# An encoder layer on one core: attention traced with priority, the input fetched a second time, gate sums and the last weight halves put into other tiles

## The chip, the cores and the metric

The kernel runs on one core of one Trainium2 chip. The metric is the device time of one execution in microseconds. TensorE (PE in the profile) multiplies matrices into PSUM, VectorE (DVE) and ScalarE (ACT) work on tiles element by element, GpSimd (POOL) and SyncE (SP) issue most of the transfers. Each engine has its own queue of instructions and works through it in order; engines wait for one another through semaphores.

## The reference

One layer of an encoder on 256 positions of width 2048, all in float32. A vector `c` sets scales, shifts and gates through one large matrix (`mod`). The layer is a windowed attention (32 query heads, 8 key and value heads of 64, rotary positions, one extra logit per head, the "sink") and an MLP with squared ReLU and 8192 hidden units; each of them is followed by a layer norm over a weighted sum with its input.

```python
c_act = jax.nn.silu(c)
mod = c_act @ mod_w[i] + mod_b[i]
sh_m, sc_m, g_m, sh_f, sc_f, g_f = jnp.split(mod, 6, axis=-1)
hmix = x * (1.0 + sc_m[:, None, :]) + sh_m[:, None, :]
y = windowed_gqa_sink(hmix, positions, attn_w_qkv[j], attn_b_qkv[j], attn_sink[j], attn_w_o[j], attn_b_o[j])
x = layer_norm(DEEPNORM_ALPHA * x + (1.0 + g_m[:, None, :]) * y, ln_mix_g[i], ln_mix_b[i])
hff = x * (1.0 + sc_f[:, None, :]) + sh_f[:, None, :]
y = sq_relu_mlp(hff, mlp_w1[i], mlp_b1[i], mlp_w2[i], mlp_b2[i])
x = layer_norm(DEEPNORM_ALPHA * x + (1.0 + g_f[:, None, :]) * y, ln_mlp_g[i], ln_mlp_b[i])
...
# inside the attention
s = jnp.where(valid[None, :, None, None], s, -jnp.inf)
m = jnp.maximum(jnp.max(s, axis=-1, keepdims=True), sk)
p = jnp.exp(s - m)
p = p / (jnp.sum(p, axis=-1, keepdims=True) + jnp.exp(sk - m))
```

With 256 positions there are two query blocks of 128, and both see all keys inside the window of 128.

## The kernel before

**Precision.** Every large product is split: a weight tile `raw` (128x2048, 1 MB) is rounded to a high part `wh` by ScalarE (L254, two halves of 128x1024 each), and VectorE takes the rest, `wl` = `raw` - `wh` (L225). Activations are split in the same way. A product is then three matmuls (`mm3`, L498 to L500: high x high, high x low, low x high), each with 512 columns. `ff_hidden` does the same with two matmuls (L1042, L1043), as its activations hold both parts side by side.

**The stream of weights.** `class Stream` holds one list of all weight tiles in order of use (`S.plan`). Its entries are either weights of a product, or tiles of the `mod` matrix, which carry a function `use` (`Mod.step`). SP loads them in this order into five buffers (`raws`; at first three more, `raws2`). `S.main()` returns the halves of the next weight tile and `pump` casts ahead of it, by up to five high halves (`NHIGH`); `S.stop` is a place in the list that `pump` does not pass. A `mod` tile is worked off either by TensorE (`quad`, L314) or by VectorE (L352, multiply and add into the tiles `part`).

**Who sets the order.** The functions are traced in a fixed order, and a planner then puts the instructions of each engine in order: among those that are ready at the time that it assumes, the one traced first goes first. A tile of a pool takes a buffer when its first writer is placed, and waits if all are taken; a buffer is free when the last reader of its tile is done.

**Pools.** `gen` has 20 buffers of 128x1024 floats (`g4()`); it holds the input `xs` (4), the projections `acc`, keys, queries, probabilities `P` and their transposes `pT`, attention outputs, hidden activations and more. `gen2` has 6 buffers of the same size (`g4b()`), opened when `raws2` is closed. PSUM has five banks `psa` (products, scores, values), two `pst` (transposes) and one `psm` (sums of `mod`).

**Stages.** First q, k, v are projected, while the input arrives, is transposed (`turn_x`) and modulated. Then come 21 steps, `n` = 0 to 20. In step `n` < 16 a block of four heads and 128 queries has its `scores` (L735, L736 on TensorE; mask and maximum L738, L740, L743, L745 on VectorE; four exponentials L749 and a small one L751 on ScalarE) and is normalised (`normalise`, L757, L758 and four L764); the block before it is transposed (`probs_T`, L774, with two copies L776), and every second step a pair of blocks is multiplied with the values (`values`, L789, cast L791). Four blocks make a group, whose queries are turned by `q_heads` (L703, L705). Beside this each step has one weight tile: the last projections in steps 0 to 3, and from step 5 on the output projection (`project`), which adds into `ys` (L849, L852) and, in its third row, adds the input `xs` (L855, L856). Step 12 makes the gate (`gate`, L391 to L398).

**The MLP** has four blocks of 2048 hidden units. For each, `ff_hidden` makes the hidden activations (in block 0 another loop, L1002 to L1029), and `ff_out` makes four columns of 512 outputs, which are added into the four tiles `ys`: in block 0 with the bias `bf` (L1081), later without (L1083). During block 1 the gate of the MLP is summed by VectorE alone (`m_gf`, L352), into two tiles `part` that are first cleared by POOL and given the bias by a DMA (L334, L335); in block 2 `gate(m_gf)` turns these sums into the gate `g2`. Block 3 ends with the fourth column: its four weight tiles are kept whole (`ws`), so that the first 128 positions can be finished, and normalised (L797 to L813, L1122 to L1129), while the second 128 are multiplied. The halves of its last two weight tiles are `kept`, in g4 tiles.

Of the kernel before, what the change touches and what calls it, by code (L numbers as in the profile page):

```python
# [12 lines left out]
F32R = mybir.dt.float32r  # L13
# [7 lines left out]
S = 256  # L21
NT = S // 128
# [8 lines left out]
BLK = 4  # L31
# [9 lines left out]
NHIGH = 5  # L41
NLOW = 5
VECS = 2
ORDER_ONLY = mybir.DependencyInfo(mybir.DependencyClass.NoSync, mybir.DependencyReason.DATA)


@with_exitstack
def hybrid_kernel(ctx: ExitStack, tc: tile.TileContext, a, out: bass.AP):
    nc = tc.nc
# [22 lines left out]
    def g4(dt=F32):  # L72
        return gen.tile([128, 1024], dt, tag="g4", name="g4")
# [96 lines left out]

        return add

    def bias_all(src, g4=g4):

        b = [g4(), g4()]
        for h in range(2):
            nc.gpsimd.dma_start(b[h], src[:, h * 1024:h * 1024 + 1024].partition_broadcast(128))
        return lambda c: b[c // 2][:, (c % 2) * 512:(c % 2) * 512 + 512]


    class Stream:
# [15 lines left out]
            self.prev = None  # L197
            self.side = {}

        def plan(self, src, use=None, kept=False):  # L200
            self.q.append((src, use, kept))

        def loads(self):
# [17 lines left out]
        def low(self):  # L221
            n = len(self.ls)
            r, kept = self.src[n]
            l = g4(F32R) if kept else wlp.tile([128, 1024], F32R, name="wl")
            self.pinned(nc.vector.tensor_sub(l, r, f32(self.hs[n])))  # L225
            self.ls.append(l)
            if n % 2:
                self.freed(self.of[n])

        def pump(self, vecs, must=0):  # L230

            while len(self.ls) < must or self.at < len(self.q):
                self.loads()
                n = len(self.hs)
                if len(self.ls) < n - 1 and len(self.ls) - self.used < self.nl or len(self.ls) < min(must, n):
                    self.low()
                    continue
                if self.at >= len(self.q) or self.at == self.stop:
                    return
                assert self.at < len(self.raw)  # L240
                src, use, kept = self.q[self.at]
                if use is not None:
                    if not vecs and n >= must:
                        return
                    vecs = max(vecs - 1, 0)
                    use(self.raw[self.at])
                    self.at += 1
                    self.freed(self.at - 1)
                    continue
                if n >= must and (n - self.used >= self.nh or kept):  # L250
                    return
                h = g4(F32R) if kept else whp.tile([128, 1024], F32R, name="wh")
                s = self.raw[self.at][:, n % 2 * 1024:n % 2 * 1024 + 1024]
                self.pinned(nc.scalar.copy(h, s))  # L254
                self.hs.append(h)
                self.src.append((s, kept))
                self.of.append(self.at)
                self.at += n % 2
# [33 lines left out]
    class Mod:  # L292
# [29 lines left out]
        def step(self, raw):  # L322
            w, kc, i = self.w, self.kc, self.i
            if i == 0:
                self.ps = psm.tile([128, 512], F32, name="pm")
            r = raw.rearrange("p (k j n) -> p k j n", k=kc // 2 if self.pairs else kc, j=4)
            self.i += 1
            last = self.i == self.n
            per = 1024 // w
            if i == self.start:  # L330

                self.part = [(g4b if self.whole else g4)() for _ in range(2)]
                for n, p in enumerate(self.part):
                    nc.gpsimd.memset(p, 0.0)  # L334
                    nc.scalar.dma_start(p[0:1], self.bias[:, n * 1024:n * 1024 + 1024])  # L335
            for k in range(kc):
                kt = i * kc + k
                if self.pairs:
                    if k % 2 == 0:
                        cols = [cact[:, kt + j // 2:kt + j // 2 + 1].to_broadcast([128, 32]) for j in range(4)]  # L340
                        self.quad(cols, [r[:, k // 2, j] for j in range(4)], last and k == kc - 2)
                elif i in self.dve:
                    e = min(4 * w, 1024)
                    new = self.part is None
                    if new:
                        self.part = [g4() for _ in range(4 * w // e)]
                    for n, p in enumerate(self.part):
                        s = raw[:, k * 4 * w + n * e:k * 4 * w + n * e + e]
                        if new:
                            nc.vector.tensor_scalar(p[:, :e], s, cact[:, kt:kt + 1], None, op0=OP.mult)  # L350
                        else:
                            nc.vector.scalar_tensor_tensor(p[:, :e], s, cact[:, kt:kt + 1], p[:, :e],  # L352
                                                           op0=OP.mult, op1=OP.add)
                else:
                    stop = last and k == kc - 1 and not self.dve
                    self.quad(cact[:, kt:kt + 1].to_broadcast([128, 32]), [r[:, k, j] for j in range(4)], stop)
            if last and not self.whole:
                if self.dve:
                    self.quad(onesf[:, :32], [self.part[j // per][:, (j % per) * w:(j % per) * w + w]
                                              for j in range(4)], True)  # L360
                self.r = sml.tile([128, 512], F32, name="mrow", bufs=2)
                nc.scalar.copy(self.r[:, :w], self.ps[:, :w])
# [116 lines left out]
    for blk in range(BLK):  # L479
        for f in range(NF):  # L480
            if blk:
                if blk == 1 and f % 2:
                    m_gf.plan()
                S.plan(a["w1b"][(blk - 1) * NF + f])
        for c in range(4):
            for kg in range(4):
                if blk == 1 and kg % 2:
                    m_gf.plan()
                S.plan(a["w2"][blk, c, kg], None, blk == BLK - 1 and c == 3 and kg > 1)


    acc, xts, held, xs = {}, {}, {}, []
# [377 lines left out]
    for h in range(2):  # L870
        qT[0, h] = q_heads(qhl[0], h)

    def mids(n):
        out = []
        if 0 < n <= 16:
            out.append(lambda: probs_T(n - 1))
        if n < 16:
            out.append(lambda: normalise(n))
        return out

    todo = []
# [1 line left out]
    for n in range(21):  # L883
        j, i = n // 4, n % 4
        if n < 16:
            scores(n)
        for f in todo:
            f()
        todo = []
        if n == 1:  # L890
            S.deep = False
        if n == 5:
            assert all(h is raws for h in S.home[S.at:]), "an early buffer is still in use"
        if n + 2 < len(LATE):
            w = qkv(*LATE[n + 2])
        elif n < 5:
            w = iter((0, 1))
        else:
            if n == 5:
                ys, bo = [g4b() for _ in range(4)], bias_all(a["bo"], g4b)  # L900
            w = project((n - 5) // 4, (n - 5) % 4)
        S.vecs(SLOT_FILL.get(n, 0) if len(LATE) - 2 <= n < 5 else 0)
        mid = mids(n)
        if j < 3:
            if i == 0:
                turn = rope(j + 1, 1)
            if i < 3:
                mid.append(lambda: qA.__setitem__(j + 1, next(turn)))
            if i == 2:
                mid.append(lambda: qhl.__setitem__(j + 1, split_q(qA[j + 1])))  # L910
            if i == 3:
                for h in range(2):
                    mid.append(lambda h=h: qT.__setitem__((j + 1, h), q_heads(qhl[j + 1], h)))
        run(w, mid)
        if 0 < n <= 16 and n % 2 == 0:
            todo.append(values(n - 1))
        if n == 12:
            g1 = gate(m_gm)
# [148 lines left out]
        return pss  # L1067

    ys = [g4b() for _ in range(4)]
    bf = bias_all(a["b2"], g4b)  # L1070
    for blk in range(BLK - 1):
        if blk:
            us = ff_hidden(blk)
        for c in range(4):
# [9 lines left out]
            if blk == 1:  # L1084
                for t in range(NT):
                    z = part(xs, t, c)
                    nc.vector.scalar_tensor_tensor(z, z, ALPHA, gb[0], op0=OP.mult, op1=OP.mult)
                    nc.vector.scalar_tensor_tensor(z, gb[1], ALPHA, z, op0=OP.mult, op1=OP.add)

    blk = BLK - 1  # L1090
    us = ff_hidden(blk)
# [120 lines left out]
```

## Time and profile before

| | us |
|---|---|
| runs of the kernel | 1139.51, 1139.80, 1135.54 (median 1139.51) |
| the profiled execution, its own time | 1136.72 |
| its span, first to last instruction | 1135.0 |
| TensorE busy in that span | 1088.9 |
| VectorE, ScalarE, GpSimd busy | 811.0, 546.7, 21.7 |

The profiled execution is one more run with the recorder on; the difference between its time and its span lies around the program. Busy time of TensorE counts pipelined matmuls, so a busy TensorE is not necessarily at its peak. A row of the profile names the line of the kernel, the engine, the operation and output<-inputs; an arrow at the end of a row gives the idle time of that engine just before it and what ended it. "Granted clock" (PEclk) is the share of the full TensorE clock that the chip allowed in that stretch.

### The profile page before, as it was taken

Reading aid. Unit: us, or ns where it says so; the run is one execution under the profiler, and the core shown is the slowest. Engines: PE = TensorE matmul, PEld = TensorE weight load, DVE = VectorE, ACT = ScalarE, POOL = GpSimd, SP = SyncE. Lnnn points to the kernel's source line nnn. Section 1 sums busy time; section 2 is a strip of 40 time slices with the busy share of each in tenths; the row PEclk is TensorE's granted clock in tenths of the full one; section 3 lists DMA queues with packets and bytes.
Section 4 is the critical chain, followed back from the end, with each engine's and each line's share of the span. In section 5 each row is a group of like instructions: output and inputs, shape, how many; then the busy total and the mean of one; then the engine's idle time right before and its main releaser. Section 6 shows DMA issues by size and latency. Waiting matters only on the chain.

```text
span 1135.0 us, 15765 instructions
## 1 busy us (share of the span) xinstructions
PE 1088.9 (96%) x6250; PEld 880.2 (78%) x6250; DVE 811.0 (71%) x1121; ACT 546.7 (48%) x852; POOL 21.7 (2%) x40
## 2 busy tenths in 40 slices
PE   8889999799999999999999999999999999999994
PEld 6657667466677699988888887878888888888883
DVE  5587896778899878765577888746666556665656
ACT  5333445676775455553444543335444344444431
POOL 2000000000000000000000010000000000000001
PEclk9999999999999999999999999999999999999997
DMA  9999995656886798655578788854555555557512
GB/s 374 419 420 418 421 392 196 253 186 255 322 305 258 276 366 313 207 187 186 196 290 296 263 303 319 303 206 155 187 187 186 185 190 193 186 187 268 200 38 75
DMA packets 42570, 288.50 MB, mean 254 GB/s; under 512 B 4720, under 2 KB 5360, under 8 KB 8704
## 3 DMA queue, kind: packets, MB, share of 16 engines
q1 hardware_dynamic: 39824, 279.85, 66.8%
q0 software_dynamic: 1792, 6.29, 1.7%
q10 hardware_dynamic: 880, 1.35, 0.3%
q8 instruction: 49, 0.80, 0.3%
q14 instruction: 25, 0.20, 0.0%
HBM read 285.38 MB, written 2.10 MB: 253 GB/s over the span
## 4 chain that ended last, share of the span: by engine, by line
PE 82%; DMA 7%; DVE 6%; ACT 3%; issue 1%; DVEq 0%; ACTq 0%; SPq 0%
PE pa L1042 15%; PE pa L498 14%; PE pa L500 14%; PE pa L499 14%; PE pa L1043 8%; DMA raw<-in_modm 4%; PE pm L314 3%; PE pa L1019 3%; PE pa L1018 3%; PE pa L1020 3%; DVE wl L225 2%; PE pa L789 1%; DMA raw<-in_wqkv 1%; PE pt L774 1%; ACT wh L254 1%
## 5 line engine op out<-in xcount | busy, mean ns | idle before, releaser
L225 DVE TENSOR_TENSOR wl<-raw,wh 128x1024 fp32r<-128x1024 f32 x332 | 404.5, 1224 | 242.0 <-ACT wh L254 241.4
L254 ACT CAST wh<-raw 128x1024 fp32r<-128x1024 f32 x332 | 348.1, 1055 | 457.9 <-PE pa L500 246.9
L498 PE MATMUL pa<-wh,g 128*128 128x512 f32 x816 | 321.5, 395 | 10.9 <-ACT g L534 3.4
L500 PE MATMUL pa<-wh,g 128*128 128x512 f32 x816 | 318.9, 392 | 1.7 <-DVE g L536 1.7
L499 PE MATMUL pa<-wl,g 128*128 128x512 f32 x816 | 319.5, 392 | 0.0
L1042 PE MATMUL pa<-g,wh 128*128 128x512 f32 x768 | 271.8, 399 | 2.9 <-DVE rl L991 2.9
L1043 PE MATMUL pa<-g,wl 128*128 128x256 f32 x768 | 215.7, 281 | 0.0
L498 PEld LDWEIGHTS pa<-wh,g 128*128 128x128 f32 x816 | 153.5, 188 | 52.0 <-issue 6.0
L500 PEld LDWEIGHTS pa<-wh,g 128*128 128x128 f32 x816 | 153.2, 188 | 38.5 <-DVE g L536 3.6
L499 PEld LDWEIGHTS pa<-wl,g 128*128 128x128 f32 x816 | 153.6, 188 | 32.6 <-issue 2.6
L1042 PEld LDWEIGHTS pa<-g,wh 128*128 128x128 f32 x768 | 144.3, 188 | 39.5 <-DVE rl L991 3.6
L1043 PEld LDWEIGHTS pa<-g,wl 128*128 128x128 f32 x768 | 145.1, 189 | 0.2
L1019 PE MATMUL pa<-g,wh 128*128 128x256 f32 x256 | 72.7, 285 | 0.4 <-DVE g L962 0.4
L1018 PE MATMUL pa<-g,wh 128*128 128x256 f32 x256 | 72.5, 286 | 0.0
L1020 PE MATMUL pa<-g,wl 128*128 128x256 f32 x256 | 72.2, 283 | 0.0
L352 DVE SCALAR_TENSOR_TENSOR g<-raw,cact,g 128x1024 f32<-128x1024 f32 x53 | 68.0, 1283 | 0.4
L314 PE MATMUL pm<-raw,cact 128*32 128x256 f32 (+2 forms) x832 | 54.8, 379 | 5.4 <-DMA raw<-in_modm 4.4
L1018 PEld LDWEIGHTS pa<-g,wh 128*128 128x128 f32 x256 | 48.7, 192 | 1.3 <-issue 0.8
L1019 PEld LDWEIGHTS pa<-g,wh 128*128 128x128 f32 x256 | 49.1, 192 | 0.9 <-DVE g L962 0.8
L1020 PEld LDWEIGHTS pa<-g,wl 128*128 128x128 f32 x256 | 49.1, 192 | 0.0
L352 DVE SCALAR_TENSOR_TENSOR g4b<-raw,cact,g4b 128x1024 f32<-128x1024 f32 x32 | 40.6, 1282 | 7.5 <-DMA raw<-in_modgf 5.2
L314 PEld LDWEIGHTS pm<-raw,cact 128*32 128x32 f32 x832 | 21.6, 109 | 27.8 <-issue 12.3
(174 smaller groups left out, 836.7 us busy)
## 6 DMA issues: line engine op xcount, KB each, us to landing
raw<-in_w SPq DMA_DIRECT2D x64, 1024.0 KB, 4.9
raw<-in_w1b SPq DMA_DIRECT2D x48, 1024.0 KB, 4.9
raw<-in_modm SPq DMA_DIRECT2D x32, 1024.0 KB, 14.7
raw<-in_modf SPq DMA_DIRECT2D x32, 1024.0 KB, 7.1
raw<-in_wqkv SPq DMA_DIRECT2D x24, 1024.0 KB, 15.2
raw<-in_modgm SPq DMA_DIRECT2D x16, 1024.0 KB, 6.0
raw<-in_wo SPq DMA_DIRECT2D x16, 1024.0 KB, 5.8
raw<-in_w1a SPq DMA_DIRECT2D x16, 1024.0 KB, 8.1
```

What stands on the lines that cost most here:

```text
L225: self.pinned(nc.vector.tensor_sub(l, r, f32(self.hs[n])))
L254: self.pinned(nc.scalar.copy(h, s))
L314: i = nc.tensor.matmul(self.ps[32 * j:32 * j + 32, :w], lhsT[j] if type(lhsT) is list else lhsT, rhs[j], start=self.first, stop=stop)
L352: nc.vector.scalar_tensor_tensor(p[:, :e], s, cact[:, kt:kt + 1], p[:, :e], op0=OP.mult, op1=OP.add)
L498: nc.tensor.matmul(ps, xh, wh, start=start, stop=False)
L499: nc.tensor.matmul(ps, xh, wl, start=False, stop=False)
L500: S.prev = nc.tensor.matmul(ps, xl, wh, start=False, stop=stop).ins
L1018: nc.tensor.matmul(o, wh(w, 128), hh, start=new, stop=False)
L1019: nc.tensor.matmul(o, wh(w, 128), hl, start=False, stop=False)
L1020: nc.tensor.matmul(o, wl(w, 128), hh, start=False, stop=end)
L1042: nc.tensor.matmul(ps, wh(k, 128), hb, start=k == 0, stop=False)
L1043: nc.tensor.matmul(ps[:, :256], wl(k, 128), hb[:, :256], start=False, stop=k == NK - 1)
```

## The change

- `first(f, ...)` traces `scores`, `normalise`, `probs_T` and `values` inside `tc.high_priority()`: for the planner their instructions stand before everything else that is ready on their engine. The subtraction that `values` returns is traced later, outside of it.
- The four input tiles `xs` are no longer used after `turn_x`. At step 9 four new g4 tiles are loaded from the same input by POOL, 512 KB each, behind the last matmul of step 9 (`AFTER`), and from then on they are `xs`.
- The gate sums `m_gf.part` of the MLP are the two tiles that hold the bias `b2` before. So that no gate sum is traced before the bias has been used, `S.stop` holds the stream at the first `modgf` tile (`first_gf`) until block 0 is through.
- The kept halves of the very last weight tile are g4b tiles; those of the last but one stay g4 tiles.

```diff
+AFTER = mybir.DependencyInfo(mybir.DependencyClass.Sync, mybir.DependencyReason.DATA)
...
-    def bias_all(src, g4=g4):
-        b = [g4(), g4()]
+    def bias_all(src, b):
         for h in range(2):
             nc.gpsimd.dma_start(b[h], src[:, h * 1024:h * 1024 + 1024].partition_broadcast(128))
...
-            l = g4(F32R) if kept else wlp.tile([128, 1024], F32R, name="wl")
+            l = (g4, g4b)[kept - 1](F32R) if kept else wlp.tile([128, 1024], F32R, name="wl")
...
-                h = g4(F32R) if kept else whp.tile([128, 1024], F32R, name="wh")
+                h = (g4, g4b)[kept - 1](F32R) if kept else whp.tile([128, 1024], F32R, name="wh")
...
-                self.part = [(g4b if self.whole else g4)() for _ in range(2)]
+                if not self.whole:
+                    self.part = [g4() for _ in range(2)]
...
                 if blk == 1 and f % 2:
+                    if f == 1:
+                        first_gf = len(S.q)
                     m_gf.plan()
...
-                S.plan(a["w2"][blk, c, kg], None, blk == BLK - 1 and c == 3 and kg > 1)
+                S.plan(a["w2"][blk, c, kg], None, max(kg - 1, 0) if blk == BLK - 1 and c == 3 else 0)
...
+    def first(f, *a):
+        with tc.high_priority():
+            return f(*a)
+
     def mids(n):
         out = []
         if 0 < n <= 16:
-            out.append(lambda: probs_T(n - 1))
+            out.append(lambda: first(probs_T, n - 1))
         if n < 16:
-            out.append(lambda: normalise(n))
+            out.append(lambda: first(normalise, n))
...
         if n < 16:
-            scores(n)
+            first(scores, n)
...
-                ys, bo = [g4b() for _ in range(4)], bias_all(a["bo"], g4b)
+                ys, bo = [g4b() for _ in range(4)], bias_all(a["bo"], [g4b(), g4b()])
...
         if 0 < n <= 16 and n % 2 == 0:
-            todo.append(values(n - 1))
+            todo.append(first(values, n - 1))
+        if n == 9:
+            for c in range(4):
+                xs[c] = g4()
+                i = nc.gpsimd.dma_start(xs[c].rearrange("p (t n) -> p t n", t=NT), a["x"][:, :, 512 * c:512 * c + 512])
+                tc.add_manual_dep(i.ins, S.prev.name, AFTER, reason="not sooner")
...
     ys = [g4b() for _ in range(4)]
-    bf = bias_all(a["b2"], g4b)
+    m_gf.part = [g4b(), g4b()]
+    bf = bias_all(a["b2"], m_gf.part)
+    S.stop = first_gf
     for blk in range(BLK - 1):
...
+        S.stop = 0
```

More of the change, by code (lines that the diff above doesn't have):

```diff
@@ L198, in __init__, with plan @@
             self.side = {}
-        def plan(self, src, use=None, kept=False):
+        def plan(self, src, use=None, kept=0):
             self.q.append((src, use, kept))
```

## The prediction

> **What bounds the kernel now.** I read the page's busy shares first, then the time cut into stretches, then the waits of TensorE, then the timelines around its gaps.
>
> ```profile
> PE 1088.9 (96%) x6250; PEld 880.2 (78%) x6250; DVE 811.0 (71%) x1121; ACT 546.7 (48%) x852; POOL 21.7 (2%) x40
> ```
>
> ```profile
> core 0: us, PE busy (x) PEld busy (x) DVE busy (x) ACT busy (x) POOL busy (x), PEclk, DMA share, GB/s
> 165.00:195.00 30.00, 29.01 (x176) 21.54 (x175) 19.12 (x29) 19.03 (x36) 1.91 (x2) 1.00 0.66 225
> 195.00:240.00 45.00, 37.10 (x183) 23.06 (x182) 32.43 (x59) 25.84 (x69) 1.25 (x2) 0.92 0.56 201
> 240.00:375.00 135.00, 134.68 (x824) 95.41 (x823) 118.54 (x197) 93.03 (x224) 1.06 (x2) 1.00 0.77 284
> 375.00:392.00 17.00, 15.59 (x138) 10.43 (x136) 15.12 (x41) 7.54 (x12) 0.95 (x1) 1.00 0.58 213
> 660.00:700.00 40.00, 37.64 (x177) 31.15 (x176) 35.09 (x43) 16.04 (x19) 4.31 (x8) 1.00 0.84 296
> 760.00:780.00 20.00, 17.13 (x94) 14.19 (x93) 13.13 (x20) 11.47 (x18) 0.00 (x0) 1.00 0.39 136
> 780.00:1095.00 315.00, 315.00 (x1596) 267.25 (x1595) 194.74 (x242) 142.11 (x176) 2.13 (x4) 1.00 0.56 191
> 1095.00:1135.00 40.00, 23.54 (x102) 18.32 (x100) 23.65 (x41) 3.97 (x6) 3.27 (x2) 0.85 0.14 53
> ```
>
> TensorE is the bound, and the change takes no matmul away. So only the holes of TensorE can be won: 7.9 us between 195 and 240, 1.0 just before, 1.4 at 375, 2.4 at 660, 2.9 at 760, and the tail, where the last engine to work is VectorE. Two answers of the wait view, one for 165 to 240 and one for 660 to 780, name what ended them:
>
> ```profile
> PE pt L703 <- ACT g L776: 3.2, 1, 3.2
> PE pt L703 <- ACT g L705: 2.3, 2, 1.3
> PE pa L498 <- DVE g L552: 2.2, 1, 2.2
> ...
> PE pa L1042 <- DVE rl L991: 2.9, 2, 2.6
> PE pa L498 <- DVE g4b L1083: 2.4, 1, 2.4
> ```
>
> Those releasers are only the last link. The timelines of ScalarE and TensorE show why they were late:
>
> ```profile
> 191.93 1.09 PE L774 MATMUL pt<-ident,g 128*128 128x128 f32 x8
> ...
> 192.44 0.21 ACT L751 ACTIVATE es<-es 128x4 f32<-128x4 f32 x1 [0.35 <-DVE es L745]
> 204.95 0.21 ACT L751 ACTIVATE es<-es 128x4 f32<-128x4 f32 x1 [8.09 <-DVE es L745]
> 209.85 0.48 ACT L749 ACTIVATE g<-pa,nm 128x256 f32<-128x256 f32 x1 [1.54 <-PE pa L500]
> 211.66 1.08 ACT L776 COPY g<-pt 128x512 f32<-128x512 f32 x2
> 212.61 1.74 ACT L764 ACTIVATE g<-g,rs 128x256 f32<-128x256 f32 x4
> 220.79 0.58 ACT L791 CAST g<-pa 128x512 fp32r<-128x512 f32 x1
> ```
>
> The small exponential of a block (L751) ran at 192.44, when its maxima were there, but its four large ones (L749) began at 209.85, and the copy of the first probability transposes (finished by 193.0) at 211.66, though ScalarE sat idle for 8.1 us in between. Both write a fresh g4 tile, and both were let go by a projection matmul (L500), which reads such tiles. So I read this as a want of g4 buffers: 20 exist, and 4 of them hold the input from the first microseconds to the end. From 209.85 on ScalarE works off the backlog, and TensorE waits for it.
>
> **The change, part by part.** *Input loaded twice.* The four g4 tiles of the input come free after their transposes and are taken again by four loads of 512 KB at step 9. In the stretch 165 to 240 that is four buffers more, against two tiles (P and its transpose) that waited. *High priority.* It moves, per block, scores, maxima, exponentials, normalisation, transposes and their copies, and per pair of blocks the values and their cast, ahead of the projection's matmuls on TensorE, the weight casts (L254) on ScalarE, and the residuals (L225) and modulation sums (L352) on VectorE; it moves no DMA, and it adds no instruction.
>
> The price of both together: at the best all holes of the stretch go, 7.9 + 1.0. The granted clock there is 0.92, so 3.6 us of full clock were missing; with TensorE busy 82% of the time I count 2.9. Together 11.8. From below, a gain of nothing, or a loss (the first rival). The nearest row is that of 240 to 375, where the work of ten of the sixteen blocks runs beside the same projections with 0.3 us of holes; by it nearly all 11.8 would come. I take 9.0 and keep 2.8 back for the changes of order that nobody has balanced.
>
> The four new loads wait on POOL for the last matmul of step 9. Behind them on that queue stand the two loads of the second bias, which nothing reads before the MLP's second matrix (its third column is added at 555.29, in a row below), so they cost nothing. What reads the reloaded input first is L856:
>
> ```profile
> 331.98 1.29 DVE L856 SCALAR_TENSOR_TENSOR g<-g,g4b 128x512 f32<-128x512 f32 x2
> ...
> raw<-in_modgf SPq DMA_DIRECT2D x16, 1024.0 KB, 6.9
> g<-in_lnrow POOLq DMA_DIRECT2D x4, 512.0 KB, 7.9
> ...
> 674.78 10.30 DMA raw<-in_modgf
> ```
>
> Step 9 lies four steps ahead of that, some 36 us (the 135 us from 240 to 375 hold about fifteen steps), against 7.9 us for such a load: nothing, while slots are free. The 2.1 MB could delay weights: at the rate of the stretch 240 to 375 (284 GB/s at a share of 0.77, so 369 GB/s full) they are 5.7 us of all DMA engines, in a stretch with 23% of 135 us, 31 us, to spare. From above, 5.7 us; from below 0; I take 0, as the spare time is five times the need. Against it speaks the Trainium skill, "DMA: Bandwidth & Descriptors", section "Issuing engines are not separate DMA queues": loads from POOL interleave on the same engines as those of SP. The trace agrees: a modulation load beside eight row loads from POOL took 10.30 us where the median is 6.9. By that rule up to four landings would come 3.4 us late each; were none hidden, the sum would be 13.6 us worse, 1133.0.
>
> *Gate sums in the tiles of the bias.* Before, the second pool of six g4b buffers is asked for seven: four sums ys, two tiles of bias, and two of gate sums, of which the first takes its slot at 383.59 and the second at 534.88, when the first bias tile is done. The fourth ys has no slot:
>
> ```profile
> 383.59 0.95 POOL L334 MEMSET g4b<- 128x1024 f32 x1 [40.29 <-issue]
> 534.88 0.96 POOL L334 MEMSET g4b<- 128x1024 f32 x1 [150.33 <-DVE g4b L1081]
> ...
> 555.29 1.28 DVE L1081 TENSOR_TENSOR g4b<-pa,g4b 128x512 f32<-128x512 f32 x2
> 560.26 1.29 DVE L352 SCALAR_TENSOR_TENSOR g4b<-raw,cact,g4b 128x1024 f32<-128x1024 f32 x1 [2.16 <-DMA g4b<-in_modgfb]
> 577.35 0.39 PE L1042 MATMUL pa<-g,wh 128*128 128x512 f32 x1
> 769.13 1.28 DVE L1081 TENSOR_TENSOR g4b<-pa,g4b 128x512 f32<-128x512 f32 x2
> 770.33 1.28 DVE L1083 TENSOR_TENSOR g4b<-g4b,pa 128x512 f32<-128x512 f32 x2
> ```
>
> The fourth column of block 0 is multiplied by 577 and added only at 769.13, when the gate has read its sums. For 192 us two of the five psa banks are held, and near the end the fourth column of block 1 holds two more. That is where the two waits of 2.4 and 2.9 us stand. With six tiles for six buffers the addition follows its matmuls, five banks are free, and both waits go: gain 5.3; bounds 0 and 5.3, and I take all of it, since between the two waits and behind them (780 to 1095) TensorE has no hole. The gate sums now start after the last bias addition, at about 580 instead of 560; one of the five raw buffers is held some 20 us longer, and VectorE, at 88% in the fullest stretch of that block (660 to 700), does the same L352 later. The stop in the queue leaves one weight tile, two halves, prepared at that border instead of up to five; a half lasts 2.7 us of matmuls (casts 2.72 apart, below) and costs 1.06 of ScalarE and 1.2 of VectorE, so they catch up while the two are used: 0. If the first sum holds VectorE for its bias load, the residuals queued behind it are late, by the 2.2 us that it waited at 560.26, less than those two halves.
>
> *Last halves in other tiles.* The end of the kernel keeps eight tiles of the last weights beside 16 others in 20 slots:
>
> ```profile
> 1105.71 1.06 ACT L254 CAST g<-raw 128x1024 fp32r<-128x1024 f32 x1 [11.18 <-PE pa L500]
> 1114.27 0.69 DVE L797 TENSOR_TENSOR tmp<-pa,g4b 128x512 f32<-128x512 f32 x1 [1.52 <-PE pa L500]
> 1119.78 0.69 DVE L797 TENSOR_TENSOR tmp<-pa,g4b 128x512 f32<-128x512 f32 x1
> 1123.38 0.68 DVE L798 TENSOR_TENSOR g<-g,tmp 128x512 f32<-128x512 f32 x1
> ...
> 1118.15 0.39 PE L500 MATMUL pa<-g,g 128*128 128x512 f32 x1
> ```
>
> A cast waited 11.2 us for a slot, so the first half's rows ended only at 1114.3, and their normalisation stands before that of the second half: its product (L797) at 1119.78, its sum (L798) only at 1123.38. With four of the eight in g4b slots that the sums have left, the first half is done 48 matmuls before the second (12 in 2.72 us, so 10.9), near 1107.3, and normalised 9.1 later (1114.27 to 1123.38), by 1117. The second half ends near 1118.0 as before (TensorE's work is the same); L797 then begins at 1118.2 and L798 at 1119.0 instead of 1123.38. Gain 4.4, bounds 0 and 5.
>
> Sum: 9.0 + 5.3 + 4.4 = 18.7. The profiled execution took 1136.7 us (span 1135.0); so 1118.0 in its terms. The median of the runs, 1139.5, is 2.8 above it; I add half of that: 1119.4.
>
> **The rivals.** *ScalarE in bursts.* The four blocks of a group become ready together. Served first, they are on ScalarE 1.8 + 0.2 + 1.7 + 1.1 + 0.3 = 5.1 us each (four L749, L751, L764, L776, half an L791), 20.4 for four, and the casts wait. Five prepared halves cover
>
> ```profile
> 1090.75 1.06 ACT L254 CAST wh<-raw 128x1024 fp32r<-128x1024 f32 x1 [1.66 <-PE pa L500]
> 1093.47 1.06 ACT L254 CAST wh<-raw 128x1024 fp32r<-128x1024 f32 x1 [1.66 <-PE pa L500]
> ```
>
> 2.72 us each, 13.6. The other 6.8 are a hole of TensorE, and as the 3.2 us hole before was followed by a low clock, 2.5 more; three later groups: 27.9, so 1147.3. It turns the result when a group costs more than 8.1. For it: nothing in the order holds scores back. Against it: ScalarE is busy 69% from 240 to 375, and banks and slots ration the blocks. By the Trainium skill, "Perfetto Trace Analysis", section "Matmuls", matmul groups should rotate through different PSUM banks; scores that take banks first would break that for the projections, and the 2.2 us wait for L552 agrees.
>
> *The slots go elsewhere, priority changes nothing.* A busy TensorE already takes the blocks in order, and other g4 tiles (rotary, q halves) fill the four slots. Then only 5.3 + 4.4 come: 1128.4.
>
> *The input comes late.* If the reload finds slots only when the last probabilities are gone, near 355, eight L856 and the last sums move behind it: about 10 us, 1129.4.
>
> **How the numbers follow.** Forecast 0.57; slots elsewhere 0.14; late input 0.05; bursts 0.24, half of them near half price (about 1134 to 1140, no change), half dearer. Half a per cent, 5.7 us, is about what can be told here. Faster 0.76, same 0.12, slower 0.12. The range: below, all of 11.8, 5.3 and 5 and the 1.4 at 375 give 1113, and the three runs lie 4 us apart, so 1109; above, through half-price bursts, 1140; the full bursts stay outside. The forecast's own range is 1112 to 1126.
>
> **What the changed profile would show.** Right: L749 of the second block within some 4 us of its L751, no hole over 2 us between 195 and 240 and a granted clock of 1.00 there; the last L1081 pair before 585 and no wait of L498 or L1042 for L1083 or L991; casts into g and g4b before 1080 of the old time scale, first L797 of the tail near its middle. Wrong: casts L254 bunched behind L749 and L764 with TensorE waiting for wh, new holes between 250 and 375, or L856 waiting for the input's load.

## The result, and the profile after

The changed kernel takes 1126.89 us (median of 4 runs, 1126.68 to 1128.31), the kernel before 1138.44 (4 runs, 1135.54 to 1139.80): a ratio of 0.9905, with a 95% interval of 0.9882 to 0.9927. The forecast was 1119.4, a gain of 19 against a median before of 1138.44; 11.5 came. The direction was right; the gain was 60% of the forecast.

First the page of the changed kernel, TensorE's line, and then its time cut into the stretches of before (columns as before: length, busy time of each engine with its count of instructions, granted clock, DMA share, GB/s).

```profile
PE 1094.9 (97%) x6250; PEld 879.8 (78%) x6250; DVE 810.3 (72%) x1121; ACT 547.6 (49%) x852; POOL 24.8 (2%) x44
```

```profile
195.00:240.00 45.00, 45.00 (x240) 28.28 (x237) 35.67 (x64) 34.42 (x87) 1.25 (x2) 1.00 0.67 240
240.00:375.00 135.00, 135.00 (x773) 90.14 (x772) 112.22 (x184) 85.43 (x198) 3.95 (x6) 1.00 0.76 285
375.00:392.00 17.00, 14.64 (x128) 9.77 (x127) 13.97 (x39) 6.17 (x9) 0.00 (x0) 0.90 0.70 258
660.00:700.00 40.00, 40.00 (x190) 33.46 (x189) 36.10 (x45) 17.12 (x20) 4.32 (x8) 1.00 0.89 316
760.00:780.00 20.00, 19.90 (x109) 16.52 (x108) 12.85 (x19) 13.11 (x21) 0.00 (x0) 1.00 0.47 161
```

The holes that the change was to close are closed: 45.00 busy of 45 from 195 to 240 with the clock at 1.00, and at 660 and 760 nothing is missing but 0.1. Yet TensorE is busy for 6 us more in all (1094.9 against 1088.9) with the same 6250 matmuls. The row to look at is the second: from 240 to 375 TensorE is busy all the time, as it was before, but starts 773 matmuls (records of all kinds) where it started 824. Busy time that does less work shows in no list of waits. And the hole at 375 has grown from 1.4 to 2.4 us, with a clock of 0.90. The wait view, for 165 to 240 and for 375 to 392, has mainly these left:

```profile
PE pa L738 <- ACT g L708: 1.0, 1, 1.0
...
PE pt L962 <- DVE g L831: 2.2, 1, 2.2
```

The timelines give the marks by which the three parts of the change can be told apart: the first matmul of the MLP, the start of its last block, the last matmul. Of the kernel before:

```profile
390.46 0.51 PE L1018 MATMUL pa<-g,wh 128*128 128x256 f32 x2
...
940.25 0.39 PE L1042 MATMUL pa<-g,wh 128*128 128x512 f32 x1
```

Of the changed kernel (later lines have numbers up to 17 higher there):

```profile
391.65 0.71 PE L1032 MATMUL pa<-g,wh 128*128 128x256 f32 x2
...
578.41 1.28 DVE L1097 TENSOR_TENSOR g4b<-pa,g4b 128x512 f32<-128x512 f32 x2
...
934.92 0.39 PE L1056 MATMUL pa<-g,wh 128*128 128x512 f32 x1
...
1101.74 0.69 DVE L800 TENSOR_TENSOR tmp<-pa,g4b 128x512 f32<-128x512 f32 x1 [7.69 <-PE pa L503]
...
1112.62 0.69 DVE L800 TENSOR_TENSOR tmp<-pa,g4b 128x512 f32<-128x512 f32 x1 [2.14 <-PE pa L503]
...
1113.35 0.69 DVE L801 TENSOR_TENSOR g<-g,tmp 128x512 f32<-128x512 f32 x1
...
1112.20 0.39 PE L503 MATMUL pa<-g4b,g 128*128 128x512 f32 x1
```

| part, from the marks | forecast | measured |
|---|---|---|
| attention: MLP begins at 390.46, then at 391.65 | 9.0 | -1.2 |
| gate sums: from there to the last block 549.8, then 543.3 | 5.3 | 6.5 |
| last block's matmuls: 177.9, then 177.3 | 0 | 0.6 |
| tail: last matmul to the end of the span 16.9, then 12.8 | 4.4 | 4.1 |
| span 1135.0, then 1125.0 | 18.7 | 10.0 |

So two terms came about as forecast, the gate sums with 1.2 us more, and the attention's is missing altogether although its holes are gone. The experiments ask where it went.

### The profile page after: what moved, and what is told of

Its sections match the earlier page's. It is cut to its first block, busy times and chain, and to the rows that moved or that the text cites. A ratio compares the mean times of both kernels' runs of the same rounds, so it can differ in the third digit from the quotient of the medians.

```text
span 1125.0 us, 15785 instructions
## 1 busy us (share of the span) xinstructions
PE 1094.9 (97%) x6250; PEld 879.8 (78%) x6250; DVE 810.3 (72%) x1121; ACT 547.6 (49%) x852; POOL 24.8 (2%) x44
## 4 chain that ended last, share of the span: by engine, by line
PE 88%; DMA 7%; DVE 3%; ACT 1%; issue 0%; DVEq 0%; SPq 0%; ACTq 0%
PE pa L1056 16%; PE pa L501 16%; PE pa L503 15%; PE pa L502 15%; PE pa L1057 8%; DMA raw<-in_modm 5%; PE pm L314 3%; PE pa L1033 3%; PE pa L1032 3%; PE pa L1034 3%; PE pa L792 2%; DMA raw<-in_wqkv 1%; PE pt L777 1%; DVE wl L225 1%; PE pa L738 1%; PE pa L739 1%
## 5 line engine op out<-in xcount | busy, mean ns | idle before, releaser
L225 DVE TENSOR_TENSOR wl<-raw,wh 128x1024 fp32r<-128x1024 f32 x332 | 403.8, 1222 | 230.8 <-ACT wh L254 230.0
L314 PEld LDWEIGHTS pm<-raw,cact 128*32 128x32 f32 x832 | 21.8, 109 | 25.4 <-issue 11.8
```

Source lines behind the costliest of these rows:

```text
L314: i = nc.tensor.matmul(self.ps[32 * j:32 * j + 32, :w], lhsT[j] if type(lhsT) is list else lhsT, rhs[j], start=self.first, stop=stop)
```

## First four runs: which part of the change does what

Theory A: priority puts score matmuls and transposes between the two value matmuls (L792) that otherwise run beside each other, so that each takes TensorE for itself. Theory B: any finer mixture of kinds costs. Theory C: the gain reaches the end of the attention and is lost in the layer norm. Theory D, a rival to the prediction's reading of the holes: it was priority that closed them, not the four buffers. Four kernels, all against the same runs of the kernel before (1139.27, median of 13); their times are in the table behind the twelve.

**Values without priority.** Edit: `todo.append(values(n - 1))` for `todo.append(first(values, n - 1))`.

> The changed kernel with the values alone traced without priority again; scores, normalisation and transposes keep it. Theory A (priority starts the first two of the four value matmuls alone, as soon as their block is transposed, so that the two 64-column halves no longer run side by side: 25.5 us of TensorE in this stretch instead of 18.9): their time returns to about 19 us, the MLP starts some 6 us sooner, and the median is 1120 to 1122. Theory B (the loss comes from finer changes between all kinds of matmuls): values alone give less than 2 us, 1125 to 1127. Theory C (the layer norm chain before the MLP swallows whatever is won earlier): the last projection ends sooner but the MLP does not start sooner, 1126 to 1127.

**No priority at all.** Edit:

```
     def first(f, *a):
-        with tc.high_priority():
-            return f(*a)
+        return f(*a)
```

> The changed kernel without any priority: the input is still fetched twice, gate sums and last halves as in the change. Theory A with the buffers as the cause of the holes: no hole over 1 us from 195 to 240, values 19 us, median 1117 to 1121. Theory D (priority, not the buffers, closed the holes): the holes of about 8 us return and the median is 1126 to 1129. Theory C: 1125 to 1127 with a longer hole before the MLP.

**No second load.** Edit: the block `if n == 9:` with its four loads is left out; priority stays.

> The changed kernel without the second load of the input: the four input tiles stay taken, priority is kept. Buffers as the cause: exponentials of the second block wait again for a tile, holes of 6 us or more from 195 to 240, and the split values on top: 1132 to 1138. Theory D: no holes, 1125 to 1128.

**Neither.** Both edits: gate sums and last halves alone.

> Only the gate sums in the tiles of the bias and the last halves in g4b tiles; attention and input as before the change. From the traces these two are worth 6.7 and 4.1 us, so 1127 to 1128 if they are all that the whole change gained; 1131 or more if part of the gain of the MLP came from the attention.

Measured: 1128.91, 1119.02, 1136.43 and 1125.22 us. The first lies above what any of the three theories gave, and the last below the 1127 to 1128 expected of it. With gate sums and last halves always in, the four corners are

| | priority | no priority |
|---|---|---|
| second load | 1126.89 (ratio 0.9905) | 1119.02 (0.9815) |
| one load | 1136.43 (0.9972) | 1125.22 (0.9878) |

The second load gains 6 to 10 us in either column, priority costs 8 to 11 us in either row, and the intervals of neighbours in a row or a column (table below) don't touch. The changed kernel and the one with neither part can't be told apart by them. Theory D falls. The exponentials of the second block show why, first without the second load but with priority, on ScalarE:

```profile
188.12 0.21 ACT L754 ACTIVATE es<-es 128x4 f32<-128x4 f32 x1 [1.34 <-DVE es L748]
...
200.39 0.21 ACT L754 ACTIVATE es<-es 128x4 f32<-128x4 f32 x1 [3.69 <-DVE es L748]
...
207.80 0.47 ACT L752 ACTIVATE g<-pa,nm 128x256 f32<-128x256 f32 x1 [1.54 <-PE pa L503]
```

then with the second load but without priority:

```profile
191.39 0.48 ACT L752 ACTIVATE g<-pa,nm 128x256 f32<-128x256 f32 x1 [0.45 <-DVE nm L746]
```

With priority alone the large exponentials still start only when a projection matmul has let go of a tile, at 207.80 as at 209.85 before, 19.7 us after their small one. With four more buffers they start when the maxima are there, without any priority. The stretches of that kernel, and the start of its MLP:

```profile
195.00:240.00 45.00, 43.77 (x237) 28.06 (x236) 37.60 (x67) 31.57 (x81) 1.25 (x2) 1.00 0.64 224
240.00:375.00 135.00, 135.00 (x812) 94.98 (x814) 117.84 (x195) 88.31 (x206) 3.94 (x6) 1.00 0.79 295
```

```profile
382.68 0.51 PE L1031 MATMUL pa<-g,wh 128*128 128x256 f32 x2
```

390.46 - 382.68 is 7.8: without priority the attention's term is there, and 812 matmuls are started where the changed kernel starts 773. So theory C's place is wrong in the main: the last matmul of the projection starts at 381.12 in the changed kernel and at 374.05 here, so 7.1 of the 9.0 us by which the MLP starts later are lost before the layer norm, and 1.9 at it.

What fills the busy time? TensorE's timeline in the changed kernel, at the first pair of values (one value matmul shows as two records, x2):

```profile
201.76 1.07 PE L792 MATMUL pa<-g,g 128*64 128x512 f32 x2
202.77 0.39 PE L738 MATMUL pa<-g,g 128*128 128x256 f32 x1
202.99 0.28 PE L777 MATMUL pt<-ident,g 128*128 128x128 f32 x1
203.20 1.07 PE L792 MATMUL pa<-g,g 128*64 128x512 f32 x2
...
204.58 1.07 PE L792 MATMUL pa<-g,g 128*64 128x512 f32 x2
...
205.96 1.07 PE L792 MATMUL pa<-g,g 128*64 128x512 f32 x2
```

and the same four without priority:

```profile
205.41 1.94 PE L792 MATMUL pa<-g,g 128*64 128x512 f32 x8
```

Four value matmuls in a row take 1.94 us; one at a time each takes 1.07, so a broken pair costs 1.07 + 1.07 - 0.97 = 1.2 us at most. Each has a weight tile of 128x64 and writes 64 of the 128 partitions of one PSUM bank, its partner the other 64 (`po[64 * s:64 * s + 64]`). By the Trainium skill, "TensorE: Matmul & The Clock Gate", section "Part 3: Packing small matmuls — row/col tiling", matmuls that fill only a part of the array can run in it at the same time; the trace agrees where partners stand next to each other (0.97 us a pair), and shows that the gain is gone as soon as one foreign matmul stands between them (1.07 us each). The groups by line, 175 to 365, for the changed kernel and for the one without priority (busy time, mean ns of one, idle before):

```profile
L792 PE MATMUL pa<-g,g 128*64 128x512 f32 x64 | 27.0, 614 | 0.0
```

```profile
L792 PE MATMUL pa<-g,g 128*64 128x512 f32 x64 | 19.8, 608 | 0.0
```

7.2 us more for the same 32 matmuls, and the spans differ by 7.7. (The 18.9 and 25.5 of the expectations count from each start to the next one's, so that nothing is counted twice. Counted so, from 149.8 to the first matmul of the MLP, the changed kernel takes 8.9 us more: 6.6 in the values, 3.2 in the same number of projection matmuls, nothing in waits, and 0.9 less in all other matmuls together. So a finer mixture costs something beyond the pairs too, as theory B has it.) Most of it would be theory A, but for the first run: with plain values the group falls to 23.2 us and the time does not fall at all. Its timeline of ScalarE and TensorE has the reason:

```profile
227.06 0.47 ACT L752 ACTIVATE g<-pa,nm 128x256 f32<-128x256 f32 x1 [4.04 <-DVE nm L746]
...
227.52 1.06 ACT L779 COPY g<-pt 128x512 f32<-128x512 f32 x2
228.15 1.53 PE L792 MATMUL pa<-g,g 128*64 128x512 f32 x4 [2.85 <-ACT g L779]
```

The value matmuls stand in fewer, longer runs in TensorE's queue (14 instead of 22), but ahead of their input: its copy waits on ScalarE behind an exponential, and that for a maximum. TensorE stands still for 2.85 us. What was saved on pairs was spent on a wait.

## Next four runs: pairs, or what fills them

**Partners reversed, no priority.** Edit, beside no priority: `for s in (1, 0):` for `for s in range(2):` in `values`.

> No high priority anywhere; second load of the input, gate sums and last halves as in the changed kernel; and in the values the partner of the later tile is traced first (s in (1, 0)), so that its partner, which is ready earlier, follows at once. In the order of instructions the 32 value matmuls then stand in 8 unbroken runs of four, against 12 runs without this edit and 22 in the changed kernel. Theory A (a value matmul without its partner beside it costs twice, and in this stage TensorE time is the time): the values' TensorE time falls from 18.9 to about 15 us and the time from 1119.0 to about 1115. Theory B (all changes of kind on TensorE cost, not this pair in particular) and theory C (what priority costs is at the seam of the layer-norm): within 1 us of 1119.

1118.13 us. The group of L792 fell to 15.5, as theory A has it, but one unbroken run waited 3.6 us for its copy:

```profile
L792 PE MATMUL pa<-g,g 128*64 128x512 f32 x64 | 15.5, 605 | 3.6 <-ACT g L779 3.6
```

The span went from 1117.3 to 1116.3 only: the wait took 3.6 of 4.3. The time is within the 1 us of 1119 that theories B and C gave; theory A's 1115 did not come.

**Priority, values and scores in traced order.** Edit, in the changed kernel, in `values` and in `scores`:

```
-                nc.tensor.matmul(...)
+                tc.keep_in_program_order(nc.tensor.matmul(...))
```

> The changed kernel with all its high priority, but the matmuls of values and scores are kept in the order in which they are traced, so that scores no longer go between two partners: 13 runs of value matmuls instead of 22, the probability transposes as scattered as before (63 groups, 66 in the changed kernel, 29 without priority). Theory A: values' TensorE time back to about 19.5 us from 25.5, the time from 1126.9 to about 1121. Theory B: what counts is the scattered transposes and projections; 1125 to 1127. Theory C: no change, 1127; and if scores now wait behind values that wait for a copy, a new hole of 2 to 3 us as in the run with plain values.

1127.87 us, no faster than the changed kernel: theory A's 1121 is wrong, and theory C's is what came, no change and a new wait of 2 to 3 us for a copy. The group, with that wait:

```profile
L792 PE MATMUL pa<-g,g 128*64 128x512 f32 x64 | 22.3, 635 | 2.3 <-ACT g L779 2.3
```

**Priority for normalisation and transposes alone.** Edit: `first` taken from `scores` and `values`.

> High priority for the normalisation and the probability transposes alone; scores and values plain; the rest as in the changed kernel. In the order of instructions 13 runs of value matmuls (12 without priority, 22 with all), 51 groups of transposes (29 and 66). Theory A: at most 1 us above the run without priority, about 1120. Theory B: the share of the scattered transposes, 22 of 37, of the 7.9 us: about 1124.

**Priority for scores alone.** Edit: `first` taken from `values`, `probs_T` and `normalise`.

> High priority for the scores alone; the rest as in the changed kernel. 14 runs of value matmuls, 28 groups of transposes. Theory A: 2 more runs at about 0.65 us each, 1120.3. Theory B: 1119, as without priority. Theory C (scores that come early hold PSUM banks and exponentials hold ScalarE, and what is left over comes late at the layer-norm): 1123 or more, with a later first matmul of the MLP.

1126.53 and 1123.43 us. The first is far above theory A's 1120 and above B's 1124 too; the second is above B's 1119 and A's 1120.3. In the first, TensorE waits 1.7 us for L831 at the layer norm, at a clock of 0.86 from 375 to 392, and 1.4 for a copy (L779); in the second TensorE waits there 1.1 us, as without priority (by the wait view for a load of `modf`), the pairs cost 2.1, and one wait for an exponential (L752) has grown from 1.2 to 2.0. Theory C's mark for the second is met, 1123 or more with a later start of the MLP (385.53 against 382.68), but not at the place that it names. So each part of the priority has a price of its own, and none of the theories gives both numbers.

## Last four runs

**Reversed, from the third tile on, no priority.** Edit: `for s in (1, 0) if n > 3 else (0, 1):`.

> As the run with reversed partners, but the first two tiles of values keep the old order (s in (1, 0) only for n > 3). There the unbroken run of four waited 3.6 us for its copy (L792 on L779 at 226), behind exponentials on ScalarE; with one matmul of it going ahead, that wait should go. Nine unbroken runs against 8 with all reversed and 12 without. Theory A (pairs are worth 0.94 us each wherever nothing else waits): values about 16 us, wait gone, span 1113 to 1114.5, time about 1115.5. Theory E (a mended pair only uncovers a wait for the copy of the transposes, so nothing is won): 1118 to 1119, and a new wait of L792 on L779 of 2 us or more elsewhere.

1116.50 us (1113.49 to 1118.99), the fastest of all and faster than both kernels. Group:

```profile
L792 PE MATMUL pa<-g,g 128*64 128x512 f32 x64 | 16.6, 606 | 1.4 <-ACT g L779 1.4
```

3.2 us of TensorE won against plain order, 1.4 of it given back as a wait; span 1114.9 against 1117.3. Theory A's span of 1113 to 1114.5 is nearly met and E's new wait of 2 us is not there. By the ratios (0.9820 and 0.9815) the two kernels can't be told apart; the 2.4 us are shown by one profiled execution each.

**Gate sums alone.** Edit: the kernel before with the tiles of `m_gf.part`, `bias_all` and `S.stop` of the change.

> The kernel before with the part for the gate sums alone (their bias and sums in the other six buffers, and the stop in the queue), last halves in the old tiles, no priority and no second load. By the prediction 5.3 us from the waits of the last block's hidden layer: about 1133.5 to 1134 where the kernel before takes 1139. If the stop moved more than that (theory F: what the edit does to the order of loads in the MLP counts too), the part for the tail would be worth less than the 4.1 us by which the traces differ after the last matmul, and this run would come below 1131.

1130.09 us, ratio 0.9937. Its stretches:

```profile
660.00:700.00 40.00, 40.00 (x189) 33.43 (x189) 35.90 (x44) 17.46 (x20) 4.31 (x8) 1.00 0.87 311
760.00:780.00 20.00, 19.90 (x109) 16.50 (x109) 13.04 (x19) 12.95 (x20) 0.00 (x0) 1.00 0.47 158
```

Both holes go, by this part alone; from the first matmul of the MLP (391.31) to its last block (934.4) it takes 543.1, 6.7 less than before. Theory F's mark of 1131 is reached: the part is worth more than 5.3. By the ratios 0.0059 are left for the tail ("neither" has 0.9878), 6.7 us, by the traces 4.1. The rest need not be the tail's: "neither" and this kernel have the same order of instructions on TensorE, VectorE and ScalarE up to 1079, and yet the first matmul of the MLP starts 2.8 us earlier in the trace of "neither" (388.56 against 391.31).

**Priority for values alone.** Edit: `first` taken from `scores`, `probs_T` and `normalise`.

> High priority for the values alone; the rest as in the changed kernel. 16 unbroken runs of value matmuls against 12 without priority, eight pairs broken against four; transposes in 27 groups as without it. Theory A: four more broken pairs at 0.94 us, about 1122.8. Theory E (what fills a broken pair would else be a wait; priority on values costs nothing, on transposes it costs): 1119 to 1120.

1123.66 us. The group of L792 takes 24.0, 4.2 more than without priority for four more broken pairs, 1.05 us each. Theory A's 1122.8 is nearly met here, with no wait in the pairs' place: theory E, by which this costs nothing, falls. From start to start the values cost 4.0 us more and the projection's matmuls 2.3, so here too the pairs are not all of it.

**Priority at the layer norm too.** Edit: `first(...)` around `add_gated`, `norm_scalars`, `normed(0, t)` of the last tile and `ff_input(0)`.

> The changed kernel with high priority also on the last tile's gated addition, its statistics, the first normalisation and the first input of the MLP (add_gated, norm_scalars, normed, ff_input(0)). In the order of instructions one cast L225 instead of two then stands between the last L800 and the first L831 on VectorE. Theory C (part of what priority costs is at the seam of the layer-norm): the wait of L962 on L831 falls from 2.2 to about 1 us and the time from 1126.9 to about 1125. Theories A and E: the same 1126.9, since PE is late there for what happened before 375.

1126.47 us, the same as the changed kernel. One of the two casts L225 did leave the chain, but the wait stayed and only changed its name:

```profile
PE pt L962 <- DVE qq L815: 2.2, 1, 2.2
```

All twelve, each against the kernel before on its chip. "Runs" are unbroken runs of the 32 value matmuls in TensorE's order (8 is the least). "Waits" are all of TensorE's in the wait view from 165 to 396 (to 402 for "no second load", whose MLP begins only at 400.68). The last two columns set each kernel against the one without priority: the sum of values, waits and missing clock ((1 - granted clock) x length, in the stretches 0 to 40, 60 to 110 and 165 to 400), and the span.

| kernel | ratio, 95% | runs | values, us | waits, us | sum | span |
|---|---|---|---|---|---|---|
| changed | 0.9905 (0.9882-0.9927) | 22 | 27.0 | 3.5 | +8.7 | +7.7 |
| values plain | 0.9906 (0.9883-0.9929) | 14 | 23.2 | 7.8 | +9.3 | +10.9 |
| no priority | 0.9815 (0.9792-0.9839) | 12 | 19.8 | 3.7 | 0 | 0 |
| no second load | 0.9972 (0.9959-0.9985) | 19 | 26.4 | 10.9 | +20.7 | +16.7 |
| neither | 0.9878 (0.9853-0.9903) | 12 | 19.8 | 10.7 | +10.7 | +5.9 |
| reversed | 0.9827 (0.9810-0.9844) | 8 | 15.5 | 7.9 | -0.1 | -1.0 |
| priority, in order | 0.9907 (0.9887-0.9927) | 13 | 22.3 | 7.3 | +9.7 | +9.7 |
| priority, transposes | 0.9896 (0.9880-0.9911) | 13 | 20.8 | 4.6 | +9.0 | +7.9 |
| priority, scores | 0.9871 (0.9851-0.9890) | 14 | 21.9 | 4.5 | +3.0 | +2.9 |
| reversed late | 0.9820 (0.9789-0.9850) | 9 | 16.6 | 5.4 | -1.5 | -2.4 |
| gate sums alone | 0.9937 (0.9919-0.9956) | | | | | |
| priority, values | 0.9886 (0.9861-0.9912) | 16 | 24.0 | 3.9 | +6.4 | +5.8 |
| priority, layer norm | 0.9913 (0.9883-0.9944) | 22 | 27.0 | 3.4 | +8.6 | +7.1 |

The sum follows the span within 1.6 us, except for the two kernels without the second load, where it is 4.0 and 4.8 too high. A part of this lies in the single executions: up to 178 us the order of instructions on TensorE, VectorE and ScalarE is the same in all of these kernels, yet one and the same `mod` matmul starts at 149.74 without priority, at 148.02 with neither, at 147.85 without the second load and at 150.78 with priority for transposes. Without priority it is

```profile
149.74 1.06 PE L314 MATMUL pm<-raw,cact 128*32 128x512 f32 x8
```

So 1.7 of the 4.8 us are won before the attention, where nothing was changed; the remainder was not settled. Differences of 1 to 3 us between two traces should be read with this in mind, and the sum as a guide, not as a proof: its terms can overlap, and it leaves out what a finer mixture costs the other matmuls.

So the price of priority is paid in several coins: broken pairs (changed kernel, values, scores), or, where they are kept whole under priority, waits for copies (plain values, in order), a little on the projection's matmuls, and a lower clock. In the changed kernel the largest part is the values (7.2 by the group's busy time, 6.6 from start to start), and the waits are as many as without priority.

The run with priority for transposes has 3.6 us of its sum from a clock of 0.96 and 0.93 before 110, where no scores exist yet (values alone: 2.0). As the order of instructions is the same there, this is of the one execution and not of the priority; at the matmul above that kernel is 1.0 us late, not 3.6. One thing stays open: the wait of 1.6 to 2.2 us at the layer norm stands in all six kernels whose normalisation and transposes have priority and in none of the others. In the kernel without the second load it comes later:

```profile
396.94 0.44 PE L956 MATMUL pt<-ident,g 128*128 128x128 f32 x2 [1.69 <-DVE g L831]
```

Taking a cast out of its chain didn't shorten the wait, and no run found its cause.

## Why the prediction was right and wrong

**The holes and their cause: right.** The want of g4 buffers was the cause, and the second load the cure, as the corners show. (Of the two rows on which the prediction read this, only that of the exponential names L500; the copy stood behind it in ScalarE's queue.) In the changed kernel ScalarE begins the second block's exponentials before the first transposes are even copied:

```profile
189.51 0.48 ACT L752 ACTIVATE g<-pa,nm 128x256 f32<-128x256 f32 x1 [1.53 <-DVE nm L746]
...
189.97 1.06 ACT L779 COPY g<-pt 128x512 f32<-128x512 f32 x2
...
192.28 0.23 ACT L754 ACTIVATE es<-es 128x4 f32<-128x4 f32 x1
```

**"The price of both together ... I take 9.0": the step that failed.** The term was mis-sized: it measured -1.2. It rested on pricing two edits by one row, and that row (240 to 375, 0.3 us of holes) counts holes only. The second load alone gives 7.8 at the MLP's start, close to the 9.0; priority then takes 9.0 away again (382.68 to 391.65), with TensorE busy all the while from 240 to 375. What failed is that priority was priced as a change of order that costs nothing but holes. The 2.8 kept back "for the changes of order" were meant for this, but were a guess between 0 and 11.8 with nothing worked out. The rows that would have given a price were in the trace of before: the value matmuls there stand in 12 runs, some in fours and some broken, and the busy time of their group shows both speeds:

```profile
L789 PE MATMUL pa<-g,g 128*64 128x512 f32 x64 | 19.8, 608 | 0.0
```

Eight whole fours of 1.94 us would be 15.5, as in the reversed run. Listing which matmuls depend on standing next to another was the missing step. The forecast without priority would have been a second case at 1119, which is what that kernel takes. By the marks, all of the gain that came lies behind the start of the MLP.

**The second load costs 0: borne out.** The four loads were issued on POOL at 286.44, landed after a median of 14.5 us, and the first reader came 46 us after the issue:

```profile
286.44 2.85 POOL L929 DMA_DIRECT2D g<-in_x  x4 [71.27 <-PE pa L503]
...
g<-in_x POOLq DMA_DIRECT2D x4, 512.0 KB, 14.5
...
332.75 0.69 DVE L859 SCALAR_TENSOR_TENSOR g<-g,g4b 128x512 f32<-128x512 f32 x1
```

The 14.5 us are almost twice the 7.9 of the row I took. By the Trainium skill, "DMA: Bandwidth & Descriptors", section "Issuing engines are not separate DMA queues", such loads share the engines with the weights, and the longer landing agrees; but no wait of TensorE for a weight appears from 165 to 396, so the 13.6 us that the rule could have cost did not come.

**Gate sums 5.3: 6.5 measured, 6.7 alone.** Both waits are gone, and the last bias pair is added at 578.41, before the 585 asked for; the stop in the queue cost nothing visible. The bound of 5.3 was a little low: it held the two waits only.

**Tail 4.4: 4.1 measured.** The first half's L800 came at 1101.74 and the second's L800 and L801 directly after each other at 1112.62 and 1113.35, as worked out. Of ScalarE's four casts into g and g4b the last came at 1081.28. The mark asked for was 1080 on the old time scale; as the last block starts 5.3 us earlier here (934.92 for 940.25), 1081.28 is 1086.6 on that scale, so the mark was missed by 6.6 us, at no cost to the tail.

**The rivals.** ScalarE in bursts did not come: no cast was missed, no hole opened between 250 and 375. "Slots elsewhere" forecast 1128.4 and lies 1.5 from the result, for a wrong reason: the slots went where they were meant to. The late input did not come. The rival that did, priority that costs TensorE time without a hole, was not among them; its nearest sentence was the one on PSUM banks, and no run here asked about banks.

## What to carry to other kernels

When a change of order is priced, count holes and also the matmuls that TensorE starts in a fully busy stretch, and ask which of its instructions are only cheap next to a partner. A high priority on an in-order queue moves a wait to the front of it: either foreign work breaks up what belongs together, or the engine stands still for the input. If buffers are what is missing, give the buffers and leave the order alone; here that was worth 8 us more by the medians, 10 by the ratios, than both together.

## What was not expected of the hardware

Two matmuls with weights of 128x64, which write the two halves of one PSUM bank, shared TensorE in these traces only where they were neighbours in its queue: 0.97 us for two, against 1.07 for each one alone.

A hole of 2.2 us, from 385.3 to 387.5, was followed by half the clock from about 388.7 on, in the changed kernel:

```profile
384.00:388.00 4.00, 1.77 (x34) 0.80 (x26) 4.00 (x17) 0.20 (x1) 0.00 (x0) 1.00 0.85 346
388.00:390.00 2.00, 1.98 (x24) 0.68 (x24) 1.19 (x6) 0.77 (x2) 0.00 (x0) 0.68 1.07 446
390.00:392.00 2.00, 1.89 (x7) 1.49 (x8) 0.36 (x1) 1.72 (x4) 0.00 (x0) 0.50 0.94 397
```

The same was seen after holes of 1.6 and 1.7 us in two of the kernels with priority (0.54 and 0.50 from 390 to 392). But after one of 1.6 us in the kernel with plain values and after one of 2.0 us with priority for scores the clock stayed at 1.00, and even after this one of 3.6 us, with partners reversed (1.00 from 195 to 240):

```profile
226.13 1.94 PE L792 MATMUL pa<-g,g 128*64 128x512 f32 x8 [3.63 <-ACT g L779]
```

So the length of a hole alone doesn't decide, and these traces give no threshold. What they agree on is the size: from 165 to 400, in each of the kernels with a lowered clock, the missing clock is about 1.7 us (half the clock for 3.4 us) or a multiple of it; holes of 1.1 us never lowered it.
